# Two-bank PSUM tiles, moved weight sums and an early first round in a Strassen-like feed-forward

## The chip, the cores and the metric

The kernel runs on one core of a Trainium2 chip. The metric is the device time of one execution, in microseconds (us); lower is better. The engines spoken of are TensorE (PE: matrix products, accumulated in PSUM), VectorE (DVE), ScalarE (ACT), GpSimd (POOL) and SyncE (SP, whose queue issues the DMAs). Each engine works through its own queue in order; semaphores order them against each other.

## The reference, cut to what matters

One decoder layer on a 1024 x 1024 activation h, all in float32. The part that the change touches is the end of it:

```python
    mixed = jax.nn.sigmoid(gate_a) * y_attn + jax.nn.sigmoid(gate_b) * y_rwkv
    h = h + mixed @ w_out
    hidden = jnp.square(jax.nn.relu(rmsnorm(h, norm2_gain) @ w_ff_in))
    return h + hidden @ w_ff_out
```

w_out is 1024 x 1024, w_ff_in 1024 x 4096, w_ff_out 4096 x 1024. Before it come the first norm, one wide input projection, banded attention and an RWKV-7 scan.

## The kernel before, in words

Everything lives transposed (features on partitions, tokens in the free dimension). A float32 product is made of three products of rounded parts (high x high, low x high, high x low), so each weight tile and each activation tile is split: ACT casts the high part (whi, thi), DVE subtracts it from the source for the low part (wlo, tlo). That is `split_w` (L930, L931) for weights and `split_t` in `rhs` (L990, L991) for hidden activations.

The output projection (L894 to L911) works on eight tiles of 128 output features. The last two (tiles 3 and 7) are done together into four PSUM tiles ps_o; `residual` adds each to h (L886), squares h on ACT and sums the squares into hs for the second norm (L888 to L892). `combos` (L820 to L857) makes from h the split right-hand sides B11, T1, T2, B21, T3, B22, T4 that the feed-forward multiplies with, each scaled by the norm's gain; the norm's 1/rms, r2, is only applied behind the ReLU.

The feed-forward runs 16 phases: eight rounds, each with a first-matrix half ("up", 512 hidden features) and a second-matrix half ("down"). A half is a Strassen-like 2 x 2 block product with seven products, P1 to P7, in the orders of line `order`: up P1 P5 P6 P2 P7 P3 P4, down P1 P5 P6 P3 P7 P2 P4. Each product is 24 matmuls of 512 columns. Step by step:

- `weight(ph, name)` is called one step ahead. It splits the weight for that product and gives POOL the block sums: a21 = a11 - a21 (L942), a11 = wa - a11 (L943), wa = a12 - a11 (L945), and for the next phase wa = a21 + a22 (L955, L962, before the first round L1064). It also issues the fetches of the next phase's blocks into buffers that have become free.
- `up` accumulates the first half's products in one PSUM tile psy of four banks (P5 and P3 in its upper two, P1, P6, P7, P4 in its lower two) and P2 in psx. ACT copies P1, P5 and P6 out to c (L1028); DVE adds P2, P7 and P3 to a c (L1034), gates it with r2 and the ReLU (L974), ACT squares it (L977); P4 goes through L1030.
- `rhs` makes the second half's right-hand sides from the squared c (L996 to L1001), and splits them.
- `down` accumulates in psx and psy, four banks each, and adds each product to h after its 24 matmuls, 2048 columns in one DVE operation (L1058); the last product of the last round goes out in four pieces.

A scheduler has fixed each engine's order beforehand, with pools deciding who waits for a free buffer. A wait is set per PSUM tile: a matmul into a tile waits for everything that still reads that tile, whichever bank it reads. At the boundary, the pool of ps_o is closed and the feed-forward's PSUM pool opened in its place, so the first feed-forward matmul waits for the last L886 add.

Of the kernel before, what the change touches and what calls it, by code (L numbers as in the profile page):

```python
# [11 lines left out]
F32 = mybir.dt.float32  # L12
F32R = mybir.dt.float32r
# [4 lines left out]
PSUM = bass.MemoryType.PSUM  # L18
# [40 lines left out]
def hybrid_block(ctx, tc, x_ap, xt_ap, win_ap, lora_ap, wbr_ap, wout_ap, wff1_ap, wff2_ap, cst_ap,  # L59
# [80 lines left out]
    def w_tile(dt, tag):  # L140
        return wpool.tile([P, NK, 128], dt, tag=tag, name=tag, bufs=2)
# [719 lines left out]
        yield  # L861

    def norm2(op, pz):
        pk = pz[:, 2, 0:16].rearrange("p (a b) -> p a b", b=2)
        pkf = pk.rearrange("p a b -> p (a b)")
        for hf in range(2):
            head_sums(pkf, 8 * hf, hs[hf])
        sm = op.tile([P, 8], F32, tag="sm", name="sm")
        V.tensor_reduce(out=sm, in_=pk, axis=AX.X, op=ALU.add)
        return newton(op, sm, 8, 1.0 / D, RMS_EPS)  # L870

    def spread(hf, rs, pz):
        rx = hs[hf].rearrange("p (a b) -> p a b", b=128)
        V.tensor_copy(out=rx, in_=rs[:, 4 * hf:4 * hf + 4].unsqueeze(2).broadcast_to([P, 4, 128]))
        pt = pz[:, 3].rearrange("p (a b) -> p a b", b=128)
# [8 lines left out]
    def residual(ct, hf, ps):  # L884
        sl = slice(hf * HALF, (hf + 1) * HALF)
        V.tensor_add(out=h[ct][:, sl], in0=h[ct][:, sl], in1=ps)  # L886
        if ct == 0:
# [10 lines left out]
    for ct in (0, 4, 1, 5, 2, 6):  # L898
        w = wout(ct)
        for hf in range(2):  # L900
            residual(ct, hf, proj(w, mh, ml, hf))
        if ct in (4, 5):
            list(combos([ct - 4], op))
    ws_ = [wout(ct) for ct in (3, 7)]
# [7 lines left out]
    list(combos([2], op))  # L912
    for j in range(4):
        residual((3, 7)[j // 2], j % 2, pss[j])
    pst.close()
    pf = ctx.enter_context(tc.tile_pool(name="pf", bufs=1, space=PSUM))
# [11 lines left out]
    def split_w(src):  # L928
        hi, lo = w_tile(F32R, "whi"), w_tile(F32R, "wlo")
        A.copy(out=hi, in_=src)  # L930
        V.tensor_sub(out=lo, in0=src, in1=hi.bitcast(F32))  # L931
        return hi, lo

    def weight(ph, name):
        def ahead(new, old):
            if ph < 15:
                nxt[new] = fetch(ph + 1, new, raw[old])

        a11, a21, a12, a22 = (raw[k] for k in ("a11", "a21", "a12", "a22"))
        w = split_w({"P1": a11, "P5": wa, "P6": a11, "P2": a12, "P7": a21, "P3": wa, "P4": a22}[name])  # L940
        if name == "P1":
            G.tensor_sub(out=a21, in0=a11, in1=a21)  # L942
            G.tensor_sub(out=a11, in0=wa, in1=a11)  # L943
        elif name == "P6":
            G.tensor_sub(out=wa, in0=a12, in1=a11)  # L945
            ahead("a21", "a11")
        elif name == "P4":
            ahead("a12", "a22")
        elif ph % 2 == 0:
            if name == "P2":  # L950
                ahead("a22", "a12")
            elif name == "P7":
                ahead("a11", "a21")
            elif name == "P3":
                G.tensor_add(out=wa, in0=nxt["a21"], in1=nxt["a22"])  # L955
        else:
# [26 lines left out]
    order = (("P1", "P5", "P6", "P2", "P7", "P3", "P4"), ("P1", "P5", "P6", "P3", "P7", "P2", "P4"))  # L983
    C, R, Z = {}, {}, {}

    def rhs(name):
        def split_t(src):
            hi = hp2.tile([P, 2, HALF], F32R, tag="thi", name="thi", bufs=2)
            lo = hp2.tile([P, 2, HALF], F32R, tag="tlo", name="tlo", bufs=2)
            A.copy(out=hi, in_=src)  # L990
            V.tensor_sub(out=lo, in0=src, in1=hi.bitcast(F32))  # L991
            R[name] = (hi, lo)

        c11, c12, c21, c22 = (C.get(c) for c in ("c11", "c12", "c21", "c22"))
        if name == "P5":
            V.tensor_sub(out=c11, in0=c12, in1=c11)  # L996
        elif name == "P6":
            V.tensor_sub(out=c11, in0=c22, in1=c11)
            V.tensor_sub(out=c12, in0=c22, in1=c12)
        elif name == "P4":  # L1000
            V.tensor_sub(out=c11, in0=c21, in1=c11)  # L1001
        split_t({"P3": c22, "P7": c12, "P2": c21}.get(name, c11))

    def up(n, name, w):
        if name == "P1":
            Z["y"] = pf.tile([P, 4, HALF], F32, tag="y", name="psy")
# [32 lines left out]
    def down(n, name, w):  # L1039
        if name == "P1":  # L1040
            Z["x"] = pf.tile([P, 4, HALF], F32, tag="x", name="psx")
        if name in ("P5", "P2"):
            Z["y"] = pf.tile([P, 4, HALF], F32, tag="y", name="psy")
# [5 lines left out]
        ps = Z["y" if name in ("P5", "P3", "P2") else "x"]  # L1049
        for c in range(4):  # L1050
            group(ps[:, c], [((hi[:, 4 * k + c], lo[:, 4 * k + c]), (th[:, k], tl[:, k])) for k in range(2)],
                  name in ("P1", "P5", "P2"))
# [123 lines left out]
```

## Time and profile before

| what | us |
|---|---|
| median of 3 runs (lowest, highest) | 1584.95 (1583.56, 1585.47) |
| profiled execution, its span | 1585.23, 1583.4 |
| last output projection matmul | 882.59 |
| first feed-forward matmul | 892.42 |
| last feed-forward matmul | 1577.15 |
| TensorE busy in the span | 1498.6 |

Start times are counted from the span's start. A round is some 85 us long; the one shown below from 1067 on is the third. "Idle" in brackets behind a row is what the engine stood still ahead of it, with what ended it.

### The profile page before, as it was taken

Reading aid. Unit: us, or ns where it says so; the run is one execution under the profiler, and the core shown is the slowest. Engines: PE = TensorE matmul, PEld = TensorE weight load, DVE = VectorE, ACT = ScalarE, POOL = GpSimd, SP = SyncE. Lnnn points to the kernel's source line nnn. Section 1 sums busy time; section 2 is a strip of 40 time slices with the busy share of each in tenths; the row PEclk is TensorE's granted clock in tenths of the full one; section 3 lists DMA queues with packets and bytes.
Section 4 is the critical chain, followed back from the end, with each engine's and each line's share of the span. In section 5 each row is a group of like instructions: output and inputs, shape, how many; then the busy total and the mean of one; then the engine's idle time right before and its main releaser. Section 6 shows DMA issues by size and latency. Waiting matters only on the chain.

```text
span 1583.4 us, 22124 instructions
## 1 busy us (share of the span) xinstructions
PE 1498.6 (95%) x8396; PEld 1176.2 (74%) x8396; DVE 1041.6 (66%) x1999; ACT 638.5 (40%) x1126; POOL 197.2 (12%) x118
## 2 busy tenths in 40 slices
PE   5999999999999999999999799998999999999998
PEld 5877767777777777788888577776777777777776
DVE  5233678889989864426655667584848485867757
ACT  6322445565555665422233333333324242323232
POOL 1000000000000000000000232222222222323220
PEclk9999999999999999999999899999999999999999
DMA  5455243333322333643341011111111111111112
GB/s 188 156 158 150 90 130 112 116 97 118 108 78 75 101 100 110 232 167 134 120 173 54 13 41 54 54 54 53 53 40 54 54 40 53 40 54 53 46 48 107
DMA packets 99769, 145.63 MB, mean 92 GB/s; under 512 B 26448, under 2 KB 48848, under 8 KB 99664
## 3 DMA queue, kind: packets, MB, share of 16 engines
q1 hardware_dynamic: 99664, 144.23, 27.7%
q8 instruction: 66, 1.08, 0.3%
q14 instruction: 39, 0.32, 0.1%
HBM read 108.54 MB, written 35.65 MB: 91 GB/s over the span
## 4 chain that ended last, share of the span: by engine, by line
PE 82%; DVE 12%; issue 2%; DMA 1%; ACT 1%; SPq 0%; DVEq 0%; ACTq 0%
PE ps_m L156 31%; PE psy L969 24%; PE psx L969 12%; DVE tlo L991 2%; PE po L156 2%; DVE wlo L931 2%; PE ps_o L911 1%; PE pu L162 1%; DVE c L1034 1%; ACT c L1028 1%; PE pk L238 1%; PE ps_s L162 1%; PE ry L636 1%; DVE h L1058 1%; PE pd L646 1%
## 5 line engine op out<-in xcount | busy, mean ns | idle before, releaser
L156 PE MATMUL ps_m<-uh,wlo 128*128 128x512 f32 x576 | 235.4, 409 | 0.0
L156 PE MATMUL ps_m<-ul,whi 128*128 128x512 f32 x576 | 234.3, 407 | 0.0
L156 PE MATMUL ps_m<-uh,whi 128*128 128x512 f32 x576 | 233.0, 404 | 0.0
L969 PE MATMUL psy<-T,whi 128*128 128x512 f32 x512 | 159.8, 393 | 0.0
L969 PE MATMUL psy<-T,wlo 128*128 128x512 f32 x256 | 103.1, 403 | 28.1 <-ACT c L1028 17.6
L156 PEld LDWEIGHTS ps_m<-uh,whi 128*128 128x128 f32 x576 | 108.6, 189 | 21.1 <-issue 0.8
L156 PEld LDWEIGHTS ps_m<-uh,wlo 128*128 128x128 f32 x576 | 108.6, 189 | 21.1 <-issue 0.6
L156 PEld LDWEIGHTS ps_m<-ul,whi 128*128 128x128 f32 x576 | 108.7, 189 | 20.2 <-issue 0.7
L969 PEld LDWEIGHTS psy<-T,whi 128*128 128x128 f32 x512 | 96.1, 188 | 21.0
L969 PE MATMUL psx<-tlo,whi 128*128 128x512 f32 x256 | 101.6, 397 | 4.1 <-DVE tlo L991 4.1
L149 DVE TENSOR_TENSOR wlo<-wraw,whi 128x512 fp32r<-128x512 f32 x101 | 67.8, 686 | 56.5 <-ACT whi L148 56.3
L969 PE MATMUL psx<-thi,wlo 128*128 128x512 f32 x256 | 101.1, 395 | 0.0
L969 PE MATMUL psx<-thi,whi 128*128 128x512 f32 x256 | 101.1, 395 | 0.0
L931 DVE TENSOR_TENSOR wlo<-fraw,whi 128x1024 fp32r<-128x1024 f32 x44 | 58.4, 1326 | 58.2 <-ACT whi L930 58.2
L991 DVE TENSOR_TENSOR tlo<-c,thi 128x1024 fp32r<-128x1024 f32 x56 | 93.4, 1668 | 0.0
L1058 DVE TENSOR_TENSOR h<-h,psx 128x2048 f32<-128x2048 f32 (+1 forms) x35 | 73.3, 2101 | 28.4 <-PE psx L969 27.9
L931 DVE TENSOR_TENSOR wlo<-wraw,whi 128x1024 fp32r<-128x1024 f32 x36 | 48.1, 1336 | 59.0 <-ACT whi L930 59.0
L969 PEld LDWEIGHTS psy<-T,wlo 128*128 128x128 f32 x256 | 48.0, 188 | 48.4 <-ACT c L1028 24.7
L969 PE MATMUL psy<-B,whi 128*128 128x512 f32 x256 | 80.8, 397 | 0.0
L148 ACT CAST whi<-wraw 128x512 fp32r<-128x512 f32 x105 | 61.0, 619 | 44.8 <-PE ps_m L156 44.7
L969 PE MATMUL psy<-tlo,whi 128*128 128x512 f32 x192 | 76.6, 399 | 2.6 <-DVE tlo L991 2.0
L969 PE MATMUL psy<-thi,wlo 128*128 128x512 f32 x192 | 75.9, 395 | 0.0
(300 smaller groups left out, 3215.5 us busy)
## 6 DMA issues: line engine op xcount, KB each, us to landing
wraw<-win SPq DMA_DIRECT2D x72, 256.0 KB, 3.3
fraw<-wff SPq DMA_DIRECT2D x32, 512.0 KB, 3.2
wraw<-wff SPq DMA_DIRECT2D x32, 512.0 KB, 3.2
gate_d<-gt SPq DMA_DIRECT2D x32, 256.0 KB, 2.0
z_d<-zt SPq DMA_DIRECT2D x24, 256.0 KB, 2.2
xt<-x SPq DMA_DIRECT2D x8, 512.0 KB, 6.0
la<-wa_d SPq DMA_DIRECT2D x8, 512.0 KB, 4.4
aq<-q_d SPq DMA_DIRECT2D x8, 512.0 KB, 4.3
```

The source lines that it names most:

```text
L148: A.copy(out=hi[:, ks], in_=raw[:, ks])
L149: (eng or V).tensor_sub(out=lo[:, ks], in0=raw[:, ks], in1=hi[:, ks].bitcast(F32))
L156: PE.matmul(out=out, lhsT=a, rhs=b, start=(n == 0), stop=(n == last))
L162: after = PE.matmul(out=out, lhsT=lhsT, rhs=rhs, start=start, stop=stop).ins
L238: PE.matmul(out=ps_out[:, col + 2 * i:col + 2 * i + 2], lhsT=sq[:, i * 128:(i + 1) * 128], rhs=c_("ind"), start=True, stop=True)
L636: PE.matmul(out=ry.rearrange("p a b -> p (a b)"), lhsT=ARf[:, cp, par], rhs=cur, start=True, stop=True)
L646: PE.matmul(out=pd, lhsT=BKt[:, c], rhs=UV[:, c], start=True, stop=True)
L911: PE.matmul(out=pss[j], lhsT=a, rhs=b[:, sl], start=(k == 0 and n == 0), stop=(k == NK - 1 and n == 2))
L931: V.tensor_sub(out=lo, in0=src, in1=hi.bitcast(F32))
L969: PE.matmul(out=out, lhsT=a, rhs=b, start=start and n == 0, stop=n == last, skip_group_check=True)
L991: V.tensor_sub(out=lo, in0=src, in1=hi.bitcast(F32))
L1058: V.tensor_add(out=ht, in0=ht, in1=ps[:, c:c + step])
```

## The change

Three things are changed. In the first half, each two-bank sum gets a PSUM tile of its own: y0, y1, x0, x1, with P1, P6, P7, P4 in y0, P5 and P3 in y1, P2 in x0; the norm's sums and the spread of r2 use x1 in the first round. The second half uses x0 with x1, or y0 with y1, for a product, and adds each tile to h as soon as its 12 matmuls are done, 1024 columns each. The weight differences a21 and a11 are given to POOL at P5 instead of P1 in the first half; the sum for the next phase at the end of the second half (line L975) moves from P2 to P4, and the buffers that the second half's fetches fill are exchanged so that a21, a11, a12, a22 go to fixed ones. For the first round, P1's weight split (w0, into buffers of c21 and c22) and the sum s1 = a21 + a22 (L929, on DVE, in the buffer of c12) are issued ahead of the last `combos`; the third and fourth residual adds stand behind the first two pieces of `combos`; the squares of tiles 3 and 7 are summed at P6.

```diff
+    w0 = split_w(raw["a11"], hp, ("c21", "c22"))
+    s1 = hp.tile([P, NK, 128], F32, tag="c12", name="s1")
+    V.tensor_add(out=s1, in0=raw["a21"], in1=raw["a22"])
+    list(combos([2], op))
+    more = combos([3], op)
+    for j in range(4):
+        res_add((3, 7)[j // 2], j % 2, pss[j])
+        if j < 2:
+            next(more)
+    pst.close()
+    pf = ctx.enter_context(tc.tile_pool(name="pf", bufs=1, space=PSUM))
...
-        w = split_w({"P1": a11, "P5": wa, "P6": a11, "P2": a12, "P7": a21, "P3": wa, "P4": a22}[name])
-        if name == "P1":
+        sm = wa if ph else s1
+        w = w0 if ph == 0 and name == "P1" else split_w({"P1": a11, "P5": sm, "P6": a11, "P2": a12, "P7": a21, "P3": wa, "P4": a22}[name])
+        if name == ("P5", "P1")[ph % 2]:
             G.tensor_sub(out=a21, in0=a11, in1=a21)
-            G.tensor_sub(out=a11, in0=wa, in1=a11)
+            G.tensor_sub(out=a11, in0=sm, in1=a11)
...
             if name == "P7":
-                ahead("a22", "a21")
+                ahead("a11", "a21")
             elif name == "P2":
-                ahead("a11", "a12")
+                ahead("a12", "a12")
+            elif name == "P4":
+                ahead("a22", "a22")
                 if ph < 15:
                     G.tensor_add(out=wa, in0=nxt["a21"], in1=nxt["a22"])
...
+    def bank(tag):
+        return pf.tile([P, 2, HALF], F32, tag=tag, name="ps" + tag)
...
         if name == "P1":
-            Z["y"] = pf.tile([P, 4, HALF], F32, tag="y", name="psy")
-            Z["x"] = pf.tile([P, 4, HALF], F32, tag="x", name="psx")
+            for b in ("y0", "y1", "x0")[:2 if n == 0 else 3]:
+                Z[b] = bank(b)
...
-        ps = {"P5": Z["y"][:, 2:4], "P3": Z["y"][:, 2:4], "P2": Z["x"][:, 0:2]}.get(name, Z["y"][:, 0:2])
+        ps = Z[{"P5": "y1", "P3": "y1", "P2": "x0"}.get(name, "y0")]
...
-        step = 1 if n == 7 and name == "P4" else 4
-        for c in range(0, 4, step):
-            ht = hall[:, r + c:r + c + step, sl]
-            V.tensor_add(out=ht, in0=ht, in1=ps[:, c:c + step])
+        step = 1 if n == 7 and name == "P4" else 2
+        for c in range(4):
+            ps = Z[xy + str(c // 2)]
+            group(ps[:, c % 2], [((hi[:, 4 * k + c], lo[:, 4 * k + c]), (th[:, k], tl[:, k])) for k in range(2)],
+                  name in ("P1", "P5", "P2"))
+            if c % step == step - 1:
+                c0 = c + 1 - step
+                ht = hall[:, r + c0:r + c + 1, sl]
+                V.tensor_add(out=ht, in0=ht, in1=ps[:, c0 % 2:c0 % 2 + step])
```

The line numbers move by the change: L931 becomes L924, L974 L987, L991 L1010, L996 L1015, L998 and L999 L1017 and L1018, L1030 L1053, L1034 L1057, L1058 L1082, and on POOL L942, L943, L945 become L953, L954, L956, and L955 and L962 L964 and L975. The order changes with it. DVE's queue where the first half of a round passes into the second, from the subtraction for P5's right-hand side on, before (h is the activation, psx and psy the sums, wlo and tlo low parts of a weight and of a right-hand side; the numbers behind c tell its four buffers apart):

```order
L996 TENSOR_TENSOR c_10361<-c_10424,c_10361 128x1024
L999 TENSOR_TENSOR c_10424<-c_10393,c_10424 128x1024
L991 TENSOR_TENSOR tlo<-c_10361,thi 128x1024
L1030 SCALAR_TENSOR_TENSOR c_10561<-psy,r_9313 128x1024
L931 TENSOR_TENSOR wlo<-wa,whi 128x1024
L998 TENSOR_TENSOR c_10361<-c_10393,c_10361 128x1024
L1058 TENSOR_TENSOR h<-h,psx 128x4x512
L931 TENSOR_TENSOR wlo<-fraw_8663,whi 128x1024
L991 TENSOR_TENSOR tlo<-c_10361,thi 128x1024
L1001 TENSOR_TENSOR c_10361<-c_10561,c_10361 128x1024
```

The same place after the change, in a round like it:

```order
L1015 TENSOR_TENSOR c_10386<-c_10449,c_10386 128x1024
L1053 SCALAR_TENSOR_TENSOR c_10586<-psy_10359,r_9316 128x1024
L924 TENSOR_TENSOR wlo<-wa,whi 128x1024
L1010 TENSOR_TENSOR tlo<-c_10386,thi 128x1024
L1082 TENSOR_TENSOR h<-h,psx_10593 128x2x512
L1017 TENSOR_TENSOR c_10386<-c_10418,c_10386 128x1024
L1082 TENSOR_TENSOR h<-h,psx_10594 128x2x512
L924 TENSOR_TENSOR wlo<-fraw_8663,whi 128x1024
L1018 TENSOR_TENSOR c_10449<-c_10418,c_10449 128x1024
L1010 TENSOR_TENSOR tlo<-c_10386,thi 128x1024
```

P6's subtractions (L999 and L998, now L1018 and L1017) have moved behind P5's tlo, and the first of them between the two halves of P1's h add. The second place is DVE's queue where the output projection ends and the feed-forward begins, before (ps_o are the last four sums, hs the sums of squares):

```order
L886 TENSOR_TENSOR h<-h,ps_o 128x512 x3
L931 TENSOR_TENSOR wlo<-fraw_8662,whi 128x1024
L892 TENSOR_TENSOR hs_8669<-hs_8669,hq 128x512
L892 TENSOR_TENSOR hs_8670<-hs_8670,hq 128x512
L886 TENSOR_TENSOR h<-h,ps_o 128x512
L892 TENSOR_TENSOR hs_8669<-hs_8669,hq 128x512
L931 TENSOR_TENSOR wlo<-wa,whi 128x1024
```

After the change (s is s1, B and tA are pieces of `combos` for tile 3):

```order
L886 TENSOR_TENSOR h<-h,ps_o 128x512 x3
L924 TENSOR_TENSOR wlo<-s_9266,whi 128x1024
L821 SCALAR_TENSOR_TENSOR B_9299<-h,vec,B_9299 128x512
L826 SCALAR_TENSOR_TENSOR tA<-h,vec,tA 128x512
L886 TENSOR_TENSOR h<-h,ps_o 128x512
L924 TENSOR_TENSOR wlo<-fraw_8662,whi 128x1024
```

The split that stands between the third and the fourth add is now P5's instead of P1's, and in place of two sums of squares two pieces of `combos` stand ahead of the fourth add.

## Rows read from the trace of the kernel before

**Rows 1.** The page's first part: busy time of each engine, share, instructions.

```profile
PE 1498.6 (95%) x8396; PEld 1176.2 (74%) x8396; DVE 1041.6 (66%) x1999; ACT 638.5 (40%) x1126; POOL 197.2 (12%) x118
```

**Rows 2.** TensorE's waits, whole span: us in total, times, longest us.

```profile
PE psy L969 <- DVE c L1034: 21.0, 16, 1.3
PE psy L969 <- ACT c L1028: 17.6, 16, 1.1
PE psy L969 <- DVE h L886: 9.4, 1, 9.4
```

**Rows 3.** Timeline, P5 in the third round: start us, us, engine, line, operation.

```profile
1074.14 0.50 PE L969 MATMUL psy<-T,wlo 128*128 128x512 f32 x1 [1.10 <-ACT c L1028]
1074.47 0.63 PE L969 MATMUL psy<-T,whi 128*128 128x512 f32 x2
1074.94 0.39 PE L969 MATMUL psy<-T,wlo 128*128 128x512 f32 x1
```

**Rows 4.** Timeline, P7's add and P3's first matmul in that round.

```profile
1097.98 1.22 DVE L1034 TENSOR_TENSOR c<-c,psy 128x1024 f32<-128x1024 f32 x1 [2.05 <-PE psy L969]
1099.26 0.50 PE L969 MATMUL psy<-B,wlo 128*128 128x512 f32 x1 [1.31 <-DVE c L1034]
```

**Rows 5.** Grouped lines of TensorE: busy us, mean ns, idle before.

```profile
L969 PE MATMUL psx<-tlo,whi 128*128 128x512 f32 x256 | 101.6, 397 | 4.1 <-DVE tlo L991 4.1
L969 PE MATMUL psy<-tlo,whi 128*128 128x512 f32 x192 | 76.6, 399 | 2.6 <-DVE tlo L991 2.0
```

**Rows 6.** Timeline, P2 of the second half: POOL's sum and DVE's tlo.

```profile
1136.99 3.30 POOL L962 TENSOR_TENSOR wa<-fraw,fraw 128x1024 f32<-128x1024 f32 x1 [16.95 <-DVE h L1058]
1137.94 3.42 DVE L991 TENSOR_TENSOR tlo<-c,thi 128x1024 fp32r<-128x1024 f32 x1
```

**Rows 7.** Windows around the start: busy us of engines, then granted clock (PEclk).

```profile
884.00:885.00 1.00, 0.00 (x0) 0.00 (x0) 1.00 (x1) 0.34 (x1) 1.00 (x1) 1.00 0.00 0
886.00:888.30 2.30, 0.00 (x0) 0.00 (x0) 2.30 (x2) 0.26 (x1) 2.30 (x1) 0.50 0.00 0
892.40:895.57 3.17, 3.15 (x7) 2.49 (x8) 3.17 (x4) 2.47 (x4) 1.24 (x1) 0.50 0.00 0
```

**Rows 8.** Timeline, from the output projection to the first P1.

```profile
882.84 2.35 POOL L1064 TENSOR_TENSOR wa<-fraw,wraw 128x1024 f32<-128x1024 f32 x1 [372.44 <-PE ps_o L911]
882.93 3.33 DVE L931 TENSOR_TENSOR wlo<-fraw,whi 128x1024 fp32r<-128x1024 f32 x1
891.69 0.67 DVE L886 TENSOR_TENSOR h<-h,ps_o 128x512 f32<-128x512 f32 x1
892.42 0.80 PE L969 MATMUL psy<-B,wlo 128*128 128x512 f32 x1 [9.43 <-DVE h L886]
```

**Rows 9.** Timeline, DVE behind P7's add, third round.

```profile
1099.12 2.63 DVE L991 TENSOR_TENSOR tlo<-c,thi 128x1024 fp32r<-128x1024 f32 x1
1102.80 1.21 DVE L931 TENSOR_TENSOR wlo<-wraw,whi 128x1024 fp32r<-128x1024 f32 x1
```

**Rows 10.** Timeline, DVE from P3's add into the second half.

```profile
1105.10 1.22 DVE L1034 TENSOR_TENSOR c<-c,psy 128x1024 f32<-128x1024 f32 x1 [1.08 <-PE psy L969]
1109.71 2.23 DVE L996 TENSOR_TENSOR c<-c,c 128x1024 f32<-128x1024 f32 x1 [1.13 <-ACT c L977]
1111.98 1.22 DVE L999 TENSOR_TENSOR c<-c,c 128x1024 f32<-128x1024 f32 x1
1113.12 1.22 DVE L991 TENSOR_TENSOR tlo<-c,thi 128x1024 fp32r<-128x1024 f32 x1
```

**Rows 11.** Timeline, DVE's last adds.

```profile
1577.58 2.48 DVE L1058 TENSOR_TENSOR h<-h,psx 128x512 f32<-128x512 f32 x4 [3.32 <-PE psx L969]
```

**Rows 12.** The page's DMA issues: KB each, median us to landing.

```profile
wraw<-wff SPq DMA_DIRECT2D x32, 512.0 KB, 3.2
xt<-x SPq DMA_DIRECT2D x8, 512.0 KB, 6.0
```

More of the change, by code (lines that the diff above doesn't have):

```diff
@@ L863, in norm2 @@
     def norm2(op, pz):
-        pk = pz[:, 2, 0:16].rearrange("p (a b) -> p a b", b=2)
+        pk = pz[:, 0, 0:16].rearrange("p (a b) -> p a b", b=2)
         pkf = pk.rearrange("p a b -> p (a b)")
@@ L874, in spread @@
         V.tensor_copy(out=rx, in_=rs[:, 4 * hf:4 * hf + 4].unsqueeze(2).broadcast_to([P, 4, 128]))
-        pt = pz[:, 3].rearrange("p (a b) -> p a b", b=128)
+        pt = pz[:, 1].rearrange("p (a b) -> p a b", b=128)
         for i in range(4):
@@ L882, in hybrid_block, with res_add, res_sq @@
     hs = [op.tile([P, HALF], F32, name=f"hs{i}") for i in range(2)]
-    def residual(ct, hf, ps):
+    def res_add(ct, hf, ps):
         sl = slice(hf * HALF, (hf + 1) * HALF)
         V.tensor_add(out=h[ct][:, sl], in0=h[ct][:, sl], in1=ps)
+    def res_sq(ct, hf):
+        sl = slice(hf * HALF, (hf + 1) * HALF)
         if ct == 0:
@@ L900, in hybrid_block @@
         for hf in range(2):
-            residual(ct, hf, proj(w, mh, ml, hf))
+            res_add(ct, hf, proj(w, mh, ml, hf))
+            res_sq(ct, hf)
         if ct in (4, 5):
@@ L911, in hybrid_block @@
                 PE.matmul(out=pss[j], lhsT=a, rhs=b[:, sl], start=(k == 0 and n == 0), stop=(k == NK - 1 and n == 2))
[L912 to L916, printed above, removed]
     for name in ("a22", "a12"):
@@ L920, in hybrid_block, with split_w @@
     hp = gst.enter_context(tc.tile_pool(name="hpool", bufs=1, side="right"))
-    more = combos([3], op)
+    def split_w(src, pool=None, tags=("whi", "wlo")):
+        hi, lo = (w_tile(F32R, t) if pool is None else pool.tile([P, NK, 128], F32R, tag=t, name=t) for t in tags)
+        A.copy(out=hi, in_=src)
+        V.tensor_sub(out=lo, in0=src, in1=hi.bitcast(F32))
+        return hi, lo
+    w0 = split_w(raw["a11"], hp, ("c21", "c22"))
+    s1 = hp.tile([P, NK, 128], F32, tag="c12", name="s1")
+    V.tensor_add(out=s1, in0=raw["a21"], in1=raw["a22"])
+    list(combos([2], op))
+    more = combos([3], op)
+    for j in range(4):
[4 more added lines that the diff above has]
+    pf = ctx.enter_context(tc.tile_pool(name="pf", bufs=1, space=PSUM))
     r2 = mpool.tile([P, T], F32, tag="m14", name="r2")
@@ L926, in hybrid_block @@
     nxt = {}
[L928 to L932, printed above, removed]
     def weight(ph, name):
@@ L946, in weight @@
             ahead("a21", "a11")
-        elif name == "P4":
-            ahead("a12", "a22")
         elif ph % 2 == 0:
@@ L955, in weight @@
                 G.tensor_add(out=wa, in0=nxt["a21"], in1=nxt["a22"])
+            elif name == "P4":
+                ahead("a12", "a22")
         else:
             if name == "P7":
-                ahead("a22", "a21")
+                ahead("a11", "a21")
             elif name == "P2":
-                ahead("a11", "a12")
+                ahead("a12", "a12")
+            elif name == "P4":
+                ahead("a22", "a22")
                 if ph < 15:
@@ L984, in hybrid_block @@
     C, R, Z = {}, {}, {}
+    def bank(tag):
+        return pf.tile([P, 2, HALF], F32, tag=tag, name="ps" + tag)
+    px1 = bank("x1")
+    Z["x0"] = bank("x0")
     def rhs(name):
@@ L1005, in up @@
         if name == "P1":
-            Z["y"] = pf.tile([P, 4, HALF], F32, tag="y", name="psy")
-            Z["x"] = pf.tile([P, 4, HALF], F32, tag="x", name="psx")
+            for b in ("y0", "y1", "x0")[:2 if n == 0 else 3]:
+                Z[b] = bank(b)
         if n == 0:
-            next(more, None)
+            if name not in ("P1", "P5"):
+                next(more, None)
             if name == "P6":
-                Z["rs"] = norm2(op, Z["x"])
+                for ct in (3, 7):
+                    for hf in range(2):
+                        res_sq(ct, hf)
+                Z["rs"] = norm2(op, px1)
             if name == "P4":
@@ L1025, in up @@
             for hf in range(2):
-                spread(hf, Z["rs"], Z["x"])
+                spread(hf, Z["rs"], px1)
         if name in ("P1", "P5", "P6"):
@@ L1039, in down @@
     def down(n, name, w):
[L1040 to L1043, printed above, removed]
+        xy = "y" if name in ("P5", "P3", "P2") else "x"
+        if name in ("P1", "P5", "P2"):
+            for b in (xy + "0", xy + "1"):
+                Z[b] = bank(b)
         hi, lo = w
@@ L1048, in down @@
             rhs(order[1][i])
[L1049 to L1052, printed above, removed]
         r, sl = dst2[name]
         end = n == 7 and name in ("P3", "P7", "P2", "P4")
-        step = 1 if n == 7 and name == "P4" else 4
-        for c in range(0, 4, step):
-            ht = hall[:, r + c:r + c + step, sl]
-            V.tensor_add(out=ht, in0=ht, in1=ps[:, c:c + step])
-            if end:
-                for ct in range(r + c, r + c + step):
-                    nc.sync.dma_start(out=out_ap[ct * P:(ct + 1) * P, sl], in_=h[ct][:, sl])
+        step = 1 if n == 7 and name == "P4" else 2
[7 more added lines that the diff above has]
+                V.tensor_add(out=ht, in0=ht, in1=ps[:, c0 % 2:c0 % 2 + step])
+                if end:
+                    for ct in range(r + c0, r + c + 1):
+                        nc.sync.dma_start(out=out_ap[ct * P:(ct + 1) * P, sl], in_=h[ct][:, sl])
     steps = [(ph, name) for ph in range(16) for name in order[ph % 2]]
-    G.tensor_add(out=wa, in0=raw["a21"], in1=raw["a22"])
     w = weight(0, "P1")
```

## Prediction

> **What bounds it now.** I read the page first: TensorE has 1498.6 us of its 1583.4 us span [rows 1], so time can only be won where it stands still, or be lost by making it stand. The table of waits sorts those standstills [rows 2]: of the waits of the feed-forward part, 21.0 us (16 waits) are for the DVE adds L1034, 17.6 us (16) for the ACT copies L1028, and one of 9.4 us is for a residual add L886 at the very start. The reader is to see that all 32 lie in the first-matrix half, four a round in eight rounds. The timeline shows what one costs [rows 3]: P5's first matmul comes with 1.10 us idle behind P1's copy, then the next start is 0.33 us later, where the steady rhythm is 0.23 with records of 0.39. So a wait loses its idle time, plus 0.39 - 0.23 = 0.16 (idle is counted from the modelled end of a record), plus 0.33 - 0.23 = 0.10 for the slow first step: idle + 0.26. Behind a DVE add the idle is 1.31 [rows 4]. The grouped lines show a second kind in the second-matrix half [rows 5]: 4.1 + 2.6 = 6.7 us idle in front of the products that want tlo. Their reason is in the timeline [rows 6]: the POOL sum L962 begins at 1136.99, and the DVE subtraction for tlo, issued at 1137.94, takes 3.42 us instead of 1.22 and ends 1.07 after POOL has (1140.29 to 1141.36). A DVE operation with two SBUF inputs waits out the POOL sum that is running.
>
> **The change, part by part.** *Two-bank tiles.* P1, P5, P6, P7, P3 and P4 go to y0 and y1 in turn, so each writes a tile that was read a whole step earlier. The 32 waits lose their reason. They cost 17.6 + 21.0 + 32 x 0.26 = 46.9 us. The h adds of the second half become two of 1024 columns for one of 2048; by the 1024-column add of [rows 4] (1.22) that is about 2.4 for 2.3 us of DVE time, beside the matmuls. The first of the two can start in mid-step, and it also holds DVE's queue there, which counts below.
>
> *Weight sums.* The sum for the next round's P3 and P5 leaves the P2 step of the second half for its last step, where it waits for a22, and the two differences move from P1 to P5 in the first half, where no tlo is made. The down stalls go: 6.7 us idle and twelve restarts (one or two a round, none in the last) x 0.26 make 9.8 us.
>
> *What is late next, first place: P4 of the first half.* I follow DVE's queue by the order. P7's add begins at 1097.98, some 0.2 after P7's last matmul, so P3 can now start at about 1097.78 and P4 24 x 0.23 = 5.53 us later, at 1103.31. But DVE's chain behind that add doesn't move: tlo for P1 stays behind POOL (2.63 us), then the gating L987 (once L974), and P4's wlo ends at 1102.80 + 1.21 = 1104.01 [rows 9]. P4 starts 0.05 after it, so 0.75 + 0.10 = 0.86 us late. In the first round the order puts wlo ahead; in seven rounds this is 6.0 us.
>
> *Second place: P6 of the second half.* P3's add (1.14 behind the start of that wlo, at 1103.94) starts a chain of split, gate, square and subtraction that before took from 1105.10 to 1111.94, 6.84 us, with POOL's difference inside it [rows 10]. So L1015 ends at 1110.78. Behind it stand, 1.14 apart [rows 10], L1053 from 1110.7, wlo and tlo for P5 (tlo ends at 1114.2; P5 starts at 1104.17 + 5.53 + 5.60 = 1115.30, 1.1 to spare). Then the order differs: before, L999 and L998 stood ahead of P1's h add; now L1017 stands between the two halves of it, and L1018 behind the next split. POOL's L956 is let go by P5's wlo at about 1113.1 and gets in when tlo has ended, at 1114.2, for 2.3 us, to 1116.5. L1017 ends 1.08 later, at 1117.6; second half of the h add 1118.7, wlo 1119.9, L1018 1121.0, tlo 1122.15. P6 would start at 1120.90 and want tlo with its second matmul, at 1121.13: late by 1.07 with the 0.05, and 0.10 for the restart, 1.17 us. Eight rounds: 9.4 us. From P3 of that half on, the same count leaves DVE 1 us and more in hand, since nothing but a split, a tlo and two h adds is due per 5.6 us.
>
> These two prices have no row of their own. From below they are zero (POOL slips through elsewhere, or the chains run a microsecond faster). From above I take one more POOL block of 2.39 us in each, the whole of the delay in [rows 6]: 8 x 2.4 = 19 us for the second place, as much for the first. I take 0.86 and 1.17, since every link has a row.
>
> *First round prepared early.* The P1 split, s1 and two POOL differences go into the output projection, where TensorE doesn't wait for DVE or ACT; I cost them at nothing. P1 itself still waits for the fourth L886 add, since its PSUM pool is let go by it. Before, that add came at 891.69 and P1 at 892.42, 9.43 us after the last matmul [rows 8]. The order after puts ahead of it: three adds, wlo of s1, L821 and L826. POOL's L956 waits for the same last matmuls as L1064 did (882.84), so wlo is blocked as its predecessor was (882.93, 3.33 us) and ends at 886.26. Three operations of about 0.67 (the fourth add's row) end at 888.3, and P1 starts there: 892.42 - 888.3 = 4.1 us won. Without the block it would be 886.3 and 6.1 us. If the clock comes back is another matter: the granted clock read 1.00 at 884 to 885 and 0.50 from 886 on, and still 0.50 from 892.40 to 895.57, in which 7 steps were made in 3.15 us instead of 7 x 0.23 = 1.6, a loss of 1.5 [rows 7]. At 888.3 it has already fallen in this trace, so I leave the 1.5 in.
>
> [...]
>
> *Tail.* Before, four adds of together 2.48 us follow the last matmul [rows 11]. Now each waits for its own chunk of six matmuls, and the next chunk in that tile waits for the add. By the order the last six matmuls would start 18 x 0.23 = 4.1 us into the step, but they wait for the second of two adds behind the sixteenth matmul: 16 x 0.23 + 0.2 + 2 x 0.62 = 5.1. So TensorE stands 1.0 us, and one add of 0.62 remains behind it instead of four: 2.48 - 0.62 - 1.0, some 0.8 won.
>
> **Sum.** -46.9 - 9.8 + 6.0 + 9.4 - 4.1 - 0.8 = -46.2. The profiled execution took 1585.23 us (span 1583.4 and 1.83 around it): 1539.0. The median of the runs lies 0.28 below the profiled one, so I expect 1538.7 us.
>
> **Rivals.** *Nothing takes the places of the old waits.* DVE is busy 66% of the span [rows 1], so there is room on average; against it, the two chains above are counted link by link, and both hang on queue order, not on load. Time: 1538.7 - 15.4 = 1523.3, and 1519.8 with the unblocked wlo and the full clock.
>
> *The turn from first to second half becomes DVE-bound.* If POOL gets in front of L1018 or tlo as well as L1017, each round loses 2.39 more: 1538.7 + 19.1 = 1557.8. For it: every DVE operation in that stretch but the h adds and L1053 has two SBUF inputs. [...] Against: only L954 and L956 are due there, and L954 is already in the 6.84 us.
>
> *The start does not do what it says.* If the fourth add stays as late as before, the 4.1 us are not won: 1542.8.
>
> *Slower than before.* The moved sum L975 can start only when a22's transfer has landed, which waits for the last split of the round; that split ends some 2.6 us into the P2 step (0.2, half an h add and the split itself, 1.2 each), transfer 0.3 + 3.2 [rows 12], sum 3.3 with a wait for DVE as in [rows 6], cast and subtraction 2.4 (the 1.21 of [rows 9] for each) give 11.8 us, and next round's P5 starts 5.6 + 5.6 + 5.53 = 16.7 after that P2: 4.9 to spare. To eat the 46.2 us it would have to be 46.2/8 = 5.8 late in each round, so a transfer of 14 us; past that the kernel is slower (1588 at 14.3). The slowest kind of 512 KB transfer on the page takes 6.0 [rows 12].
>
> **How the numbers follow.** The forecast, new waits of 5 to 22 us in all, 1530 to 1546: 0.58, its own time 1538.7. Nothing in place, 1519 to 1530: 0.16. DVE-bound turn, 1546 to 1566: 0.19. No gain at the start alone, 1542.8: 0.03. Slower: 0.02, and no change 0.02, the old waits in new places to the same sum. Nothing within 0.2% (3.2 us, about what a measurement of this kernel can tell from no change) comes from any likelier case, so faster has 0.96. The range leaves out the lower half of the second case and the upper half of the third: 1523 to 1555.
>
> **What would show it.** In the profile after, waits of TensorE for copies and adds of the first half must be gone; if some 20 us of them stand, the tiles are still tied together. P4 there should wait for wlo by some 0.7 us, P6 of the second half for tlo by about 1 us, in every round, and L1017 should last over 2 us beside POOL's L956. No tlo wait should stand at P2 or P4 of the second half. The first feed-forward matmul should come 5 to 6 us after the last ps_o one, at granted clock 0.50. I am wrong if the second half shows waits at P5, or at P1 and P5 of the first half: then the splits or a22 are late, and the time is over 1550.

## The result and the profile after

| what | before | after |
|---|---|---|
| median of 4 runs each (lowest, highest), us | 1585.05 (1583.56, 1585.47) | 1538.47 (1537.76, 1539.05) |
| profiled execution, its span, us | 1585.23, 1583.4 | 1539.05, 1537.3 |
| last output projection matmul to first feed-forward matmul, us | 9.83 | 5.72 |
| first to last feed-forward matmul, us | 684.73 | 644.10 |
| span behind the last feed-forward matmul, us | 6.25 | 4.5 |

The changed kernel is faster: ratio 0.9708, 95% interval 0.9691 to 0.9724. The three stretches of the table account for the span: -4.1, -40.6 and -1.8, with +0.4 because the output projection ended 0.4 later in this execution (its last matmul lies between 880.81 and 883.10 in the traces of this case, at 880.89 in a second trace of the changed kernel), give -46.1, and the spans differ by 46.1.

The page's first part, which answers to [rows 1] (busy time, share of the span, instructions):

```profile
PE 1491.2 (97%) x8396; PEld 1179.0 (77%) x8396; DVE 1039.3 (68%) x2055; ACT 638.9 (42%) x1126; POOL 195.3 (13%) x117
```

TensorE's waits over the whole span, as in [rows 2] (us in total, times, longest us):

```profile
PE psx L982 <- DVE tlo L1010: 7.3, 8, 1.6
PE psy L982 <- DVE h L886: 5.3, 1, 5.3
PE psy L982 <- DVE wlo L924: 4.4, 7, 0.6
...
PE psx L982 <- DVE h L1082: 0.9, 1, 0.9
```

What matters is what is missing: the 21.0 and 17.6 us for adds and copies to c are gone, all 32 of them. In their place stand 8 waits for tlo, one a round, and 7 for wlo, one in each round but the first. The timeline of the third round places them. Columns as in [rows 3]; DVE, POOL and the matmuls that wait, with the rows of other work left out:

```profile
1080.63 1.22 DVE L1057 TENSOR_TENSOR c<-c,psy 128x1024 f32<-128x1024 f32 x1 [2.04 <-PE psy L982]
...
1081.77 2.66 DVE L1010 TENSOR_TENSOR tlo<-c,thi 128x1024 fp32r<-128x1024 f32 x1
1084.35 1.21 DVE L987 SCALAR_TENSOR_TENSOR c<-c,r 128x1024 f32<-128x1024 f32 x1
1085.48 1.21 DVE L924 TENSOR_TENSOR wlo<-wraw,whi 128x1024 fp32r<-128x1024 f32 x1
...
1086.75 0.50 PE L982 MATMUL psy<-T,wlo 128*128 128x512 f32 x1 [0.62 <-DVE wlo L924]
...
1095.65 1.22 DVE L1010 TENSOR_TENSOR tlo<-c,thi 128x1024 fp32r<-128x1024 f32 x1
1095.86 3.28 POOL L956 TENSOR_TENSOR wa<-wraw,fraw 128x1024 f32<-128x1024 f32 x1 [3.48 <-DVE wlo L924]
1096.78 1.21 DVE L1082 TENSOR_TENSOR h<-h,psx 128x1024 f32<-128x1024 f32 x1
1097.91 2.30 DVE L1017 TENSOR_TENSOR c<-c,c 128x1024 f32<-128x1024 f32 x1
1100.14 1.21 DVE L1082 TENSOR_TENSOR h<-h,psx 128x1024 f32<-128x1024 f32 x1
...
1101.27 1.21 DVE L924 TENSOR_TENSOR wlo<-fraw,whi 128x1024 fp32r<-128x1024 f32 x1
1102.41 1.21 DVE L1018 TENSOR_TENSOR c<-c,c 128x1024 f32<-128x1024 f32 x1
1103.54 1.21 DVE L1010 TENSOR_TENSOR tlo<-c,thi 128x1024 fp32r<-128x1024 f32 x1
...
1104.81 0.50 PE L982 MATMUL psx<-tlo,whi 128*128 128x512 f32 x1 [0.81 <-DVE tlo L1010]
```

Down to 1086.75 it is the first half, from P7's add on: tlo (blocked by POOL, 2.66), gate and wlo follow each other as in [rows 9], P3 no longer waits for the add, and P4 starts 0.06 behind wlo's end. From 1095.65 on it is the second half. L956 is let go by P5's wlo, waits out tlo (which ends at 1096.87) and ends at 1099.14; L1017, issued at 1097.91, ends 1.07 behind it, as tlo did in [rows 6], and takes 2.30 instead of 1.21. The add to h at 1096.78 has one input in PSUM and takes its usual 1.21 beside the same POOL operation. Behind L1017 DVE doesn't catch up before P6 wants tlo.

From the output projection to the first P1, in answer to [rows 8]:

```profile
883.29 2.36 POOL L956 TENSOR_TENSOR wa<-wraw,fraw 128x1024 f32<-128x1024 f32 x1 [21.60 <-PE ps_o L915]
...
883.33 3.40 DVE L924 TENSOR_TENSOR wlo<-s,whi 128x1024 fp32r<-128x1024 f32 x1
...
887.98 0.68 DVE L886 TENSOR_TENSOR h<-h,ps_o 128x512 f32<-128x512 f32 x1
...
888.71 4.58 PE L982 MATMUL psy<-B,c 128*128 128x512 f32 x12 [5.32 <-DVE h L886]
```

And three windows there, as in [rows 7] (the stretch and its length, busy us of PE, PEld, DVE, ACT, POOL, then the granted clock):

```profile
885.00:886.00 1.00, 0.00 (x0) 0.00 (x0) 1.00 (x1) 1.00 (x3) 0.65 (x1) 1.00 0.00 0
886.00:888.70 2.70, 0.00 (x0) 0.00 (x0) 2.70 (x5) 0.92 (x3) 0.00 (x0) 1.00 0.00 0
888.70:892.20 3.50, 3.49 (x8) 2.79 (x9) 3.50 (x6) 2.31 (x5) 0.00 (x0) 0.51 0.38 136
```

The fourth add ends at 888.66, P1 starts on it. The clock reads 1.00 through the whole gap and 0.51 once TensorE is at work again; 8 steps took 3.50 us where 8 x 0.23 = 1.84 would do. When the clock falls differs between executions; the section on the prediction comes back to it.

### The profile page after: what moved, and what is told of

It reads as the page before. It is cut to its first block, busy times and chain, and to the rows that moved or that the text cites. A ratio compares the mean times of both kernels' runs of the same rounds, so it can differ in the third digit from the quotient of the medians.

```text
span 1537.3 us, 22192 instructions
## 1 busy us (share of the span) xinstructions
PE 1491.2 (97%) x8396; PEld 1179.0 (77%) x8396; DVE 1039.3 (68%) x2055; ACT 638.9 (42%) x1126; POOL 195.3 (13%) x117
## 4 chain that ended last, share of the span: by engine, by line
PE 76%; DVE 18%; issue 2%; DMA 2%; ACT 1%; SPq 0%; DVEq 0%; ACTq 0%
PE ps_m L156 31%; PE psy L982 17%; PE psx L982 12%; DVE wlo L924 2%; PE po L156 2%; PE ps_o L915 1%; PE pu L162 1%; DVE h L1082 1%; DVE c L987 1%; DVE tlo L1010 1%; DVE c L1057 1%; DVE c L1015 1%; DVE c L1017 1%; PE pk L238 1%; PE ps_s L162 1%
## 5 line engine op out<-in xcount | busy, mean ns | idle before, releaser
L924 DVE TENSOR_TENSOR wlo<-fraw,whi 128x1024 fp32r<-128x1024 f32 x47 | 62.3, 1326 | 62.8 <-ACT whi L923 62.8
L1082 DVE TENSOR_TENSOR h<-h,psx 128x1024 f32<-128x1024 f32 (+1 forms) x66 | 78.0, 1183 | 20.3 <-PE psx L982 20.0
L953 POOL TENSOR_TENSOR fraw<-fraw,fraw 128x1024 f32<-128x1024 f32 x16 | 43.0, 2686 | 348.4 <-DVE s L929 347.3
L923 ACT CAST whi<-fraw 128x1024 fp32r<-128x1024 f32 x47 | 49.2, 1046 | 82.3 <-PE psx L982 57.3
L1010 DVE TENSOR_TENSOR tlo<-c,thi 128x1024 fp32r<-128x1024 f32 x56 | 78.2, 1397 | 2.2 <-ACT thi L1009 2.2
L982 PE MATMUL psy<-thi,whi 128*128 128x512 f32 x192 | 75.7, 395 | 0.0
```

Of the source, the lines that this page charges most:

```text
L982: PE.matmul(out=out, lhsT=a, rhs=b, start=start and n == 0, stop=n == last, skip_group_check=True)
L1082: V.tensor_add(out=ht, in0=ht, in1=ps[:, c0 % 2:c0 % 2 + step])
```

## Experiments

The theory: the gain is the 32 tile waits and the tlo stalls of the second half, and what is left of it is set by two chains on DVE's queue (P4 of the first half waits for wlo behind tlo and gate; P6 of the second waits for tlo because L1017 meets POOL's L956) and by the place of the fourth residual add. Rivals: the new waits come from the moved sums or from the early start, not from the tiles; or DVE is simply too full at the turn. The kernel before took 1586.99 us beside the first four runs, 1586.68 beside the next four, 1585.08 beside the last three. "FFN" is first to last feed-forward matmul in the profile, which the noise of the earlier stages doesn't touch: 684.73 before, 644.10 after.

**One part of the change at a time, on the kernel before.** Tiles alone:

```diff
-        ps = {"P5": Z["y"][:, 2:4], "P3": Z["y"][:, 2:4], "P2": Z["x"][:, 0:2]}.get(name, Z["y"][:, 0:2])
+        ps = Z[{"P5": "y1", "P3": "y1", "P2": "x0"}.get(name, "y0")]
...
-        step = 1 if n == 7 and name == "P4" else 4
+        step = 1 if n == 7 and name == "P4" else 2
```

> The kernel before with the two-bank tiles of both halves alone. My theory: the 32 waits for copies and adds go (-46.9), the last step wins 0.8, and the two new waits come with it, since they need neither the moved sums nor the early start: 0.9 us at P4 in seven rounds (+6.3) and 1.1 at P6 in eight (+9.5 with the longer first one). The old tlo waits at P2 and P4 of the second half stay (9.8). That is 1585.0 - 31.9 = 1553.1. Rival, DVE has room enough and the new waits come from the moved sums: 1537.3 and no wait at P4 and P6.

Measured: 1546.13 us, ratio 0.9737 (0.9713 to 0.976); FFN 648.55, so 36.2 us less. TensorE's waits:

```profile
PE psx L969 <- DVE tlo L997: 9.5, 14, 1.6
PE psy L969 <- DVE h L886: 9.4, 1, 9.4
PE psy L969 <- DVE wlo L931: 4.4, 7, 0.6
```

Both new waits are here without the moved sums and without the early start (8 of the 14 tlo waits are P6's, the other 6 old ones of P2 and P4), so they come with the tiles, and the first rival falls. But the time is some 7 us under what was expected: counted by the starts of the matmuls, the old stalls at P2 and P4 of the second half cost 10.0 us in the kernel before and only 4.2 here. The timeline shows why, at the end of a second half, where [rows 6] have the like (there at P2, here at P4):

```profile
1200.92 1.22 DVE L1065 TENSOR_TENSOR h<-h,psy 128x1024 f32<-128x1024 f32 x1
...
1207.78 3.46 POOL L942 TENSOR_TENSOR fraw<-fraw,fraw 128x1024 f32<-128x1024 f32 x1 [4.42 <-DMA fraw<-wff]
...
1208.89 3.42 DVE L997 TENSOR_TENSOR tlo<-c,thi 128x1024 fp32r<-128x1024 f32 x1
...
1212.37 0.51 PE L969 MATMUL psx<-tlo,whi 128*128 128x512 f32 x1 [0.20 <-DVE tlo L997]
```

In the kernel before, the same place of the same round, the fourth, looked so:

```profile
1219.76 2.29 DVE L1058 TENSOR_TENSOR h<-h,psy 128x2048 f32<-128x2048 f32 x1 [1.04 <-PE psy L969]
...
1227.77 3.44 POOL L942 TENSOR_TENSOR fraw<-fraw,fraw 128x1024 f32<-128x1024 f32 x1 [4.37 <-DMA fraw<-wff]
...
1228.88 3.42 DVE L991 TENSOR_TENSOR tlo<-c,thi 128x1024 fp32r<-128x1024 f32 x1
...
1232.35 0.50 PE L969 MATMUL psx<-tlo,whi 128*128 128x512 f32 x1 [0.83 <-DVE tlo L991]
```

P4's tlo waits out POOL's L942 and takes 3.42 us in both, but TensorE waits 0.20 instead of 0.83. L942 waits for a transfer, which is issued (at 1204.46 here, at 1224.51 before) as soon as DVE has split P2's weight, and that split stands in DVE's queue behind P3's add to h. In the kernel before, the one add of 2048 columns stood 1.04 us for P3's last matmul, and the queue followed it without a gap; of the two adds that the tiles make of it, the second begins at 1200.92 without a wait. So L942 begins 1.57 us behind P2's first matmul (1206.21) instead of 2.61 (1225.16), and P4's tlo ends 1.04 earlier against TensorE's work; 0.39 of that the kernel before had already lost by a stall in P2. The tiles alone take away more than half of the stalls that the moved sums are to remove.

Sums alone:

```diff
-        if name == "P1":
+        if name == ("P5", "P1")[ph % 2]:
...
             if name == "P7":
-                ahead("a22", "a21")
+                ahead("a11", "a21")
             elif name == "P2":
-                ahead("a11", "a12")
+                ahead("a12", "a12")
+            elif name == "P4":
+                ahead("a22", "a22")
                 if ph < 15:
                     G.tensor_add(out=wa, in0=nxt["a21"], in1=nxt["a22"])
```

> The kernel before with the POOL weight sums moved alone. My theory: the tlo waits of the second half go and nothing else changes, 1585.0 - 9.8 = 1575.2, and the table of waits shows no tlo at all. Rival, the sums only change their victims (a POOL sum holds another DVE operation that a step waits for): 1582 to 1588.

Measured: 1574.96, ratio 0.9921 (0.9902 to 0.994); FFN 675.08, 9.65 us less, beside 9.8 in the prediction. The waits for c stand untouched and no row for tlo is left:

```profile
PE psy L971 <- DVE c L1036: 21.0, 16, 1.3
PE psy L971 <- ACT c L1030: 17.6, 16, 1.1
```

Early start alone:

```diff
+    w0 = split_w(raw["a11"], hp, ("c21", "c22"))
+    s1 = hp.tile([P, NK, 128], F32, tag="c12", name="s1")
+    V.tensor_add(out=s1, in0=raw["a21"], in1=raw["a22"])
...
-    G.tensor_add(out=wa, in0=raw["a21"], in1=raw["a22"])
```

> The kernel before with the early first round alone. My theory: the gap between output projection and feed-forward shrinks from 9.4 to about 5.3 us, the granted clock is still at half for the first 3 us of the feed-forward, 1585.0 - 4.1 = 1580.9. Rival, the work put into the output projection costs there what the start wins: 1585.

Measured: 1580.13, ratio 0.995 (0.9931 to 0.997), with the wait for L886 at 5.3 us instead of 9.4 and FFN 685.34, unchanged within a microsecond:

```profile
PE psy L980 <- DVE h L886: 5.3, 1, 5.3
```

So the FFN parts alone are -36.2 (tiles), -9.65 (sums) and +0.6 (start), together -45.2, where all three at once give -40.6. With the tiles in place the sums are worth some 4.5 us (648.55 to 644.10, early start included), close to the 4.2 of old stalls that the tiles alone leave.

**The wait at P6.** The kernel after without POOL's L956 in the second half; P3 there multiplies with a stale sum.

```diff
-            G.tensor_sub(out=wa, in0=a12, in1=a11)
+            if ph % 2 == 0:
+                G.tensor_sub(out=wa, in0=a12, in1=a11)
```

> The changed kernel without the POOL difference a12 - a11 (L956) in the second halves; P3 there then multiplies with a stale sum. My theory: L1017 lasts 1.2 instead of over 2 us and P6 no longer waits for tlo in rounds 2 to 8; all 9.5 us of these waits but at most 1 us of the first round go: 1538.5 - 9 = 1529.5. Rival, P6 waits because of the two operations put ahead of its tlo, whatever POOL does: 1538.5 with the waits unchanged.

Measured: 1530.47, ratio 0.9639 (0.9621 to 0.9657); FFN 635.45, 8.65 less than after. L1017's counterpart takes its plain time:

```profile
1095.98 1.21 DVE L1018 TENSOR_TENSOR c<-c,c 128x1024 f32<-128x1024 f32 x1
```

and P6's wait stands in the first round alone, with 0.5 us. So without the meeting of L956 and L1017 seven of P6's eight waits don't arise.

The same wait can go without leaving anything out. L1018, the second subtraction, isn't needed before P7. Here it is issued for P7:

```diff
         elif name == "P6":
             V.tensor_sub(out=c11, in0=c22, in1=c11)
+        elif name == "P7":
             V.tensor_sub(out=c12, in0=c22, in1=c12)
```

> The changed kernel with L1018 (c12 for P7) taken out of the way of P6's tlo and issued for P7. My theory: the wait at P6 is a chain of DVE operations, and one link of 1.14 us less ends it: the seven waits of 1.09 and about 1.1 of the first round's 1.87 go, 644 - 8.7 = 635.4 us in the feed-forward, the whole 8.7 below the changed kernel. Rival, only POOL's block counts and the freed slot is filled by another wait: no change.

Measured: 1530.34, ratio 0.9636 (0.9614 to 0.9659), beside a second run of the kernel after:

> The changed kernel once more, as the measure for the three others of this call: 0.971 of the kernel before; feed-forward 644 us from its first to its last matmul; P4 of the first half waits 0.6 us for wlo in seven rounds and P6 of the second 0.8 us for tlo in seven, 1.6 in the first.

That was 1537.98 (ratio 0.9685, 0.9662 to 0.9707). So 7.6 us less, for one DVE operation of 1.14 us moved out of the chain; the wait for tlo is down to 0.4, once. That is 1.1 us a round out of a chain that was 1.0 late (a step of 1.21 for 0.23).

**The wait at P4.** The split of P4's weight ahead of the gate of P7's c:

```diff
+        if "gate" in Z:
+            act2(Z.pop("gate"), 1)
...
-            act2(c, 0 if name == "P2" else 1)
+            if n and name == "P7":
+                Z["gate"] = c
+            else:
+                act2(c, 0 if name == "P2" else 1)
```

> The changed kernel with P4's split of the first half put ahead of the gate L987 of P7's sum in DVE's queue. My theory: the wait of P4 goes (7 x 0.90), but DVE's chain from P7's add to P6's tlo keeps its length, so P6 waits as much longer, 1.9 instead of 1.0 us: no change of the time, 644 us in the feed-forward, within 1 us. Rival, the two waits are independent: 6.3 us less.

Measured: 1552.47, ratio 0.9775 (0.975 to 0.98): 14.5 us slower than after_again, a miss. P4's wait is gone, but TensorE's other waits have grown:

```profile
PE psx L982 <- DVE tlo L1010: 13.5, 8, 1.7
...
PE psy L982 <- DVE tlo L1010: 3.1, 7, 0.5
```

Two reasons show in its timeline. First, ACT. The late gate makes the square of c late, and it stands in ACT's queue ahead of the cast of the next P1 weight:

```profile
1085.87 1.06 ACT L990 ACTIVATE c<-c 128x1024 f32<-128x1024 f32 x1 [5.02 <-DVE c L987]
...
1086.83 1.03 ACT L923 CAST whi<-fraw 128x1024 fp32r<-128x1024 f32 x1
1087.89 1.23 DVE L924 TENSOR_TENSOR wlo<-fraw,whi 128x1024 fp32r<-128x1024 f32 x1 [0.93 <-ACT whi L923]
...
1104.95 0.51 PE L982 MATMUL psx<-tlo,whi 128*128 128x512 f32 x1 [1.71 <-DVE tlo L1010]
```

DVE stands 0.93 us for the cast, in the middle of the chain that sets P5 and P6: from P7's add to the end of P5's tlo it takes 17.25 us, where the kernel after takes 16.24 for the same operations in another order. Second, the clock: in four of seven rounds it fell behind these waits. Windows of the third round, from the first wait on:

```profile
1102.70:1105.00 2.30, 0.53 (x3) 0.24 (x2) 2.30 (x3) 1.99 (x2) 0.00 (x0) 1.00 0.53 155
1106.00:1109.00 3.00, 3.00 (x9) 2.32 (x8) 3.00 (x4) 0.00 (x0) 0.00 (x0) 0.53 0.00 0
1109.00:1112.00 3.00, 3.00 (x15) 2.43 (x14) 1.59 (x2) 0.00 (x0) 0.00 (x0) 1.00 0.00 0
```

9 matmuls in 3 us at a granted clock of 0.53, 15 in the next 3 us at 1.00. A round without the drop took 80.8 us, one with it 82.4, one of the kernel after 79.83.

Next, late_c12 and late_gate together, with some DVE operations ordered by hand: L1017 behind both of P1's adds to h and ahead of P6's weight split, L1018 and P5's adds behind P6's tlo (cut to the adds and L1017). (`issue_after` puts an operation behind the named one in its engine's queue; `t6` is P6's tlo.)

```diff
-                V.tensor_add(out=ht, in0=ht, in1=ps[:, c0 % 2:c0 % 2 + step])
+                with tc.issue_after(Z["t6"]) if name == "P5" else nullcontext():
+                    add = V.tensor_add(out=ht, in0=ht, in1=ps[:, c0 % 2:c0 % 2 + step]).ins
+                if name == "P1" and c == 3:
+                    with tc.issue_after(add):
+                        Z["c6"] = V.tensor_sub(out=C["c11"], in0=C["c22"], in1=C["c11"]).ins
```

> Both of these, and L1017 put behind both h adds of P1 and ahead of P6's split, so that POOL's L956 runs beside the two adds that read PSUM, and P5's h adds behind P6's tlo. My theory: L1017 is blocked by under 1.1 us, P6's tlo ends 0.4 us before it is wanted with P4 on time, and both waits go: 644 - 13.9 - 1 = 629 us in the feed-forward, 15 below the changed kernel. Rival, DVE is simply full at this turn: at least 4 us of the waits stay, now at P5 or P3 of the second half.

Measured: 1529.32, ratio 0.9632 (0.9605 to 0.9659), 8.7 less than after_again where 15 were hoped for. P4 and P6 are gone from the table of waits, but P5 waits 0.5 to 0.6 for its tlo in seven rounds, with the same late cast in the chain (17.25 us from P7's add). turn2 keeps all of that but runs the deferred gate behind P3's gate, so its square no longer stands in the cast's way (the edit against turn, cut):

```diff
-        if "gate" in Z:
-            act2(Z.pop("gate"), 1)
...
+            if name == "P3" and "gate" in Z:
+                act2(Z.pop("gate"), 1, last)
```

> The second version of the turn: P7's gate L987 (and the square behind it on ACT) not merely behind P4's split but behind P3's gate, where DVE waits for a square anyway. My theory: in the first version the square of c22 pushed ACT's cast of P1's weight 0.9 us back, and P5's tlo came 0.5 us late for it; with the square behind P3's the cast is early, P5's tlo ends 0.4 us before it is wanted, and no wait of the turn is left: 7 x 0.7 less than the first version, 630 us in the feed-forward, 1524. Rival, L987 of c22 meets POOL's L954 there and P5 or P6 is late by 1 us or more: 1529 or above.

Measured: 1526.72, ratio 0.9628 (0.9605 to 0.9652); FFN 632.89. The table of waits has no row for wlo or tlo of the feed-forward left. The same chain takes 16.91 us, and P5's slow step falls from 0.83 and more to 0.49; it is not gone, and 630 us were expected. turn2 takes the gate out of the way of P3's add on DVE too, so how much of this gain is ACT's the two runs don't separate. late_gate is the clearer case: 0.93 of the 1.01 us that its chain is longer is DVE standing for the cast.

**The start.** The blocked split of P5's weight (883.33 above; its predecessor is in [rows 8]) stands ahead of the fourth add. Here the add is issued first:

```diff
-        res_add((3, 7)[j // 2], j % 2, pss[j])
+        last_add = res_add((3, 7)[j // 2], j % 2, pss[j]).ins
...
+                                                                  after=last_add if ph == 0 and name == "P5" else None)
```

> The changed kernel with the fourth residual add put ahead of the split of s1 in DVE's queue, so that the blocked split no longer holds the add that lets the first P1 go. My theory: the first feed-forward matmul comes about 1.2 us after the last ps_o one instead of 5.7, and, since the granted clock reads 1.00 for 2 us after a last matmul, it stays at 1.00: 4.5 + 1.5 = 6 us less, 1532. Rival, B113 or P5's split are then late and take the time back in P1 or P5: 1536 to 1538.

Measured: 1531.55, ratio 0.9661 (0.9642 to 0.968). The gap to the first feed-forward matmul is 1.18 us for 5.72, and the clock stays:

```profile
881.60:882.50 0.90, 0.12 (x2) 0.06 (x1) 0.88 (x3) 0.90 (x3) 0.90 (x1) 1.00 0.00 0
882.50:886.00 3.50, 3.50 (x15) 2.87 (x16) 3.50 (x3) 2.35 (x5) 1.46 (x1) 1.00 0.00 0
```

15 steps in 3.50 us, where the kernel after made 8. By the profiles 6.3 us are won, 4.54 in the gap and 1.76 in the FFN (642.34) behind it, where 1.66 were lost to the clock.

**Both together,** turn2 with the fourth add first:

> The second version of the turn and the early fourth add together. My theory: the two don't touch, 1524 - 6 = 1518; TensorE's waits in the feed-forward are then only the last step's 0.9 us. Rival, the first round's order shifts with the earlier start and its steps P5 and P6 wait: 1521 or more.

Measured: 1519.57 (1519.05 to 1521.06), ratio 0.9587 (0.9567 to 0.9607), 18.9 under the median of the kernel after; FFN 630.49. It beats both kernels. TensorE's waits from the boundary on:

```profile
PE psx L985 <- DVE h L1094: 0.9, 1, 0.9
PE psy L985 <- DVE h L886: 0.8, 1, 0.8
```

What is left in seven rounds is a slow step of 0.49 at P5 and one of 0.28 at P6, each with one of 0.34 behind it, 3.7 us in all: P5's tlo is still a little late, below what the table lists. DVE and POOL still meet at the deferred gate, in the chain to that tlo; whether the slow steps would go without it no run shows:

```profile
1077.53 3.26 POOL L957 TENSOR_TENSOR fraw<-wa,fraw 128x1024 f32<-128x1024 f32 x1 [5.30 <-DVE wlo L925]
...
1078.44 3.43 DVE L992 SCALAR_TENSOR_TENSOR c<-c,r 128x1024 f32<-128x1024 f32 x1
```

## Why the prediction was right

The predicted 1538.7 us met 1538.47. The mechanism held, each term to about half a microsecond; that the total is met to 0.2 is luck, since single executions of this kernel spread over 1.3 us (1537.76 to 1539.05). Point by point:

- *The 32 waits, 46.9 us, and the tlo stalls, 9.8.* Both sets are gone from the table. The sums alone gave 9.65. The 46.9 have no run of their own, since every kernel with the tiles also has the new waits. Step by step in the trace before, the 32 waits cost 47.3 us and the tlo stalls 10.0; the FFN total (predicted -46.9 - 9.8 + 6.0 + 9.4 + 1.0 = -40.3, measured -40.6) agrees.
- *P4 waits for wlo, 0.86 in seven rounds.* Start to start it was 1.02 and 0.34 in place of two times 0.23: 0.90, in the seven rounds foretold.
- *P6 waits for tlo, 1.17 in eight.* L956 and L1017 met, L1017 took 2.30, and P6 lost 1.09 (steps of 1.21 and 0.34) in seven rounds and 1.87 in the first. In sum the two places lost 15.8 us where 15.4 were predicted. L956 slipped in behind P5's tlo, the place that the prediction gave it.
- *The start, 4.1.* The gap is 4.11 shorter, for the reason given: the blocked split (3.40), then three short operations.
- *The tail.* Each of the four chunks has its add, and the last six matmuls start 1.2 us late for 1.0:

```profile
1530.19 1.28 DVE L1082 TENSOR_TENSOR h<-h,psx 128x512 f32<-128x512 f32 x2 [1.76 <-PE psx L982]
1531.53 0.50 PE L982 MATMUL psx<-thi,wlo 128*128 128x512 f32 x1 [0.91 <-DVE h L1082]
...
1533.24 0.69 DVE L1082 TENSOR_TENSOR h<-h,psx 128x512 f32<-128x512 f32 x1 [1.76 <-PE psx L982]
```

Three things in the working did not hold, though none changed the sum.

- *The clock.* I left 1.5 us in because "at 888.3 it has already fallen in this trace". In the profiled execution after it had not: it read 1.00 up to the restart and 0.51 behind it, and 1.66 us were lost. In after_again, the same kernel with its restart at 886.61, it had fallen inside the gap, as I had read it off the kernel before:

```profile
884.00:886.60 2.60, 0.00 (x0) 0.00 (x0) 2.60 (x5) 0.81 (x3) 0.00 (x0) 0.50 0.00 0
```

So it had in nine more traces with a gap of 5.7 us or more, the kernel before among them, 2.5 to 4.3 us after the start of the last matmul, and the restart lost 1.6 to 2.3 us by the starts of the matmuls. The reason that I gave is thus the common case, and the profiled execution the exception. A full clock behind the restart, which would have saved 1.5 us, was met in none of these eleven traces; only add_first and final2, which closed the gap to 1.18 us, kept the clock. As far as the granted clock's rows tell, the moment isn't fixed by the idle time alone: no fall was seen in the 5.3 us of idle of the profiled execution after, while in the kernel before, for one, the clock read 0.50 from 886.00 on, 3.4 us after the last matmul [rows 7].
- *Terms that overlap.* The sum added 9.8 for the moved sums to 46.9 for the tiles. It was right for both together, but not as a price of each: tiles alone won 36.2 where my terms gave 30.5 (46.9 - 6.0 - 9.4 - 1.0), because two adds to h in place of one already free DVE's queue, the next transfer and POOL's difference earlier (tiles_only above). I had priced that split add at nothing and looked only for harm in it.
- *How thin the chains are.* I counted DVE's queue alone. late_gate showed that ACT's queue is as tight at the turn: one square in front of one cast held DVE for 0.93 us, and P5 and P6 came late.

Of the rivals, "nothing in place" (1523.3) failed as the chains said, though a few moved operations reach 1526.72, which shows that queue order, not DVE's load (68% after), set the new waits. The DVE-bound turn (1557.8) didn't come: at the turn POOL blocked L1017, but neither L1018 nor tlo. The moved sum was never late.

## What to carry to other kernels

A dependency kept per tile makes a matmul wait for a reader of another bank, here 32 times with 38.6 us of idle; when a table of waits shows the bounding engine waiting for copies out of PSUM at every step, give each sum a tile of its own, then follow the queue of the engine that did those copies link by link, for the next wait stands there. Two parts of a change that shorten the same queue must be priced together, in the order in which they are applied. Where a POOL operation delays such a queue, taking an operation that isn't due yet out of the queue can be worth as much as taking POOL's away: here 8.3 us of FFN time (644.70 to 636.40) against 8.65.

## What was not expected of the hardware

- The clock fell in late_gate without any long idle: gaps of 0.84, 0.46 to 0.49 and 2.18 us start to start, with matmuls between them, and then 6 or 7 steps of 0.43 us. It did so in four of seven rounds with the same instructions. What decides it the runs don't show.
- POOL and DVE excluded each other only where the DVE operation has two SBUF inputs: L1017 with two took 2.30 beside POOL's L956, the add to h with one PSUM input 1.21. In the whole feed-forward after, 34 DVE operations of 128x1024 with one PSUM input ran beside a POOL operation, and none took over 1.22. It goes in both directions: L956, let go while P5's tlo ran, ended 2.27 us behind it, and L1017 ended 1.07 behind L956. In the same stretch, in all 35 cases in which a DVE operation with two SBUF inputs was issued while a POOL operation ran, it ended 1.07 to 1.09 us behind POOL's; in all 33 in which the DVE operation was first, POOL's ended 2.25 to 2.28 behind it.
